# Constant products in the waits of four layer normalisations of a decoder step

## The chip, the cores and the metric

The kernel runs on one core of a Trainium2 chip. The metric is the time of one execution on the device in microseconds (us), as the median of several runs. All inputs and outputs lie in the chip's memory, in float32.

## The reference

One step of a two-layer decoder. Layer 0 is a convolution module and an MLP; layer 1 is attention with stick-breaking weights and an MLP. Both run for a prompt of 512 tokens and for 8 samples of 4 tokens with 2048 past keys each. Every sub-layer ends in the same normalisation:

```python
def post_norm_residual(x, y, gate, g, b):
    return layer_norm(DEEPNORM_ALPHA * x + (1.0 + gate) * y, g, b)

def layer_norm(x, g, b):
    mu = mean(x, -1);  var = mean(square(x - mu), -1)
    return (x - mu) * rsqrt(var + LN_EPS) * g + b
...
h = x * (1.0 + scale) + shift            # ahead of each sub-layer
y = square(relu(h @ mlp_w1)) @ mlp_w2    # the MLP
```

The convolution module has a `layer_norm` of its own between its depthwise convolution and its last projection. The model's width is 1024, the MLP's 4096.

## The kernel before

The prompt's activations lie transposed: eight tiles `v` of 128 channels by 512 tokens. A dense layer multiplies 128 x 128 blocks of weights with these tiles into a PSUM bank `pd`. For precision every factor is split into a high and a low part (`whi`, `wlo`, `xhi`, `xlo`, or `h2h`, `h2l` in the MLP), and `mm3` issues three products for each pair of blocks, in lines 311, 314 and 315. `wsplit` makes the parts of the weights, `split` and `make_h` those of the activations.

A normalisation has to work across channels, which lie across partitions. `Norm.add` transposes each finished tile of `v` by TensorE into a bank `lnT` (line 350), and VectorE takes its statistics (`bn_stats`). After the last tile `Norm.bands` does three things. It aggregates the statistics. It spreads the mean over all partitions: `spread` makes diagonal matrices `dg` out of the means (on VectorE for the even blocks of 128 tokens, on ScalarE for the odd ones) and multiplies them by `onesm`, a matrix of ones, into a bank `mb`. And it works out the reciprocal deviation by a Newton iteration of small VectorE instructions (`rstd_of`) and spreads that into a bank `rb` in the same way. In line 370 stand all these products. `make_h` then subtracts `mb` from each tile and multiplies it by `rb` (lines 404 and 405, VectorE), makes `xhi` and `h` on ScalarE (lines 438 and 440) and `xlo` on VectorE (line 444).

Four normalisations of the prompt are concerned. They are called here C (in the convolution module, object `cnrm`), 0A (behind the convolution module), 0B (behind the first MLP) and 1A (behind the attention). C and 0B treat all 512 tokens at once. 0A and 1A go in two halves of 256 tokens (`H_0A = H_1A = 1`), with mean and deviation of a half side by side in one bank `mrb`. The first half is normalised while the last tiles of the second half are still being made, and its first products, 48 of 256 columns in `p_tiles`, are issued as soon as `make_h` has its tiles; `second_half` starts the second half's.

Two streams of work are interleaved, the prompt's and the samples' (`ada_A`, `sd_acc`, `w_acc`, `zt`, `av` belong to the latter), by a clock of costs that the generators yield. Behind that a scheduler puts the instructions of each engine into one order, by a simulated time line, priorities (the statistics run under `high_priority`) and dependences through tiles; `order` adds a dependence between two instructions that has no semaphore and sets the order alone. The banks of PSUM are three for `pm` (products, and `mrb` of a first half or `rb`), four for `aux`, and one for `ln`.

Of the kernel before, what the change touches and what calls it, by code (L numbers as in the profile page):

```python
# [17 lines left out]
P = 128  # L18
# [92 lines left out]
def yoco_step_kernel(  # L111
# [10 lines left out]
    mm = nc.tensor.matmul  # L122
    tr = nc.tensor.transpose
# [17 lines left out]
    def pm(name="pm"):  # L141
        return ps.tile([P, 512], F32, tag="pm", bufs=3, name=name)
# [30 lines left out]
    ident = c1[:, 0:128]  # L173
# [5 lines left out]
    onesm = base.tile([P, P], F32, name="onesm")  # L179
# [40 lines left out]
    pt = aux("pt_c")  # L220
# [96 lines left out]
    def order(ins, after):  # L317
        tc.add_manual_dep(ins.ins, after.ins.name,
                          mybir.DependencyInfo(mybir.DependencyClass.NoSync, mybir.DependencyReason.DATA), reason="issue order")
        return ins  # L320
# [16 lines left out]
    axd = [dr.tile([KT, P, T], F32, name=f"axd{i}") for i in range(2)]  # L337

    class Norm:
        def __init__(self, n=4, pl4=None, psum=None):  # L340
            self.n, self.psum, self.first, self.after = n, psum, None, None
            self.st = pp.tile([P, 4, KT, 6], F32, tag="bn", bufs=1, name="bn") if n == 4 else pl4.tile(
                [P, n, KT, 6], F32, tag="bn2", bufs=2, name="bn2")

        def add(self, v, k, ts=None, keep=None):
            blocks = range(self.n) if ts is None else range(ts.start // P, ts.stop // P)
            with tc.high_priority(LN_PRI):
                pt = (self.psum or lnp)("lnT")
                for i in blocks:
                    tr(pt[:, i * P : i * P + P], v[:, i * P : i * P + P], ident)  # L350
                for i in blocks:
                    vec.bn_stats(self.st[:, i, k, :], pt[:, i * P : i * P + P])  # L352
            if keep is not None:
                for i in blocks:
                    nc.scalar.copy(keep[i], pt[:, i * P : i * P + P])
# [21 lines left out]
        def bands(self, ts):  # L377
            if self.first and ts.start == 0:
                return self.first
            b0, b1 = ts.start // P, ts.stop // P  # L380
            with tc.high_priority(LN_PRI):
                mv = self.aggregate(range(b0, b1))
                if b1 - b0 == 4:
                    mb, rb = lnp("mb"), pm("rb")
                else:
                    both = (lnp if b0 else pm)("mrb")
                    mb, rb = both[:, 0:256], both[:, 256:512]
                self.spread(mv[:, b0:b1, 0], mb)
                self.spread(rstd_of(mv[:, b0:b1, 1], b1 - b0), rb)
                return mb, rb  # L390

    ALL = slice(0, T)

# [14 lines left out]
    last_spread = []  # L408

    def rstd_of(var, n):  # L410
        ve = stmp([P, 32], "ve", tag="ln0")[:, 0:n]
        vh = stmp([P, 32], "vh", tag="ln3")[:, 0:n]
        y = stmp([P, 32], "rs", tag="ln1")[:, 0:n]
        w = stmp([P, 32], "rw", tag="ln2")[:, 0:n]
        vec.tensor_scalar_add(ve, var, EPS)
        vec.tensor_scalar(w.bitcast(I32), ve.bitcast(I32), 1, None, op0=ALU.logical_shift_right)
        vec.tensor_scalar(y.bitcast(I32), w.bitcast(I32), -1.0, float(0x5F3759DF), op0=ALU.mult, op1=ALU.add)
        vec.tensor_scalar_mul(vh, ve, -0.5)
        for _ in range(3):
            vec.tensor_tensor(w, y, y, op=ALU.mult)  # L420
            vec.tensor_tensor(w, w, vh, op=ALU.mult)
            last_rstd[:] = [vec.scalar_tensor_tensor(y, w, 1.5, y, op0=ALU.add, op1=ALU.mult)]
        return y
# [175 lines left out]
    for h in range(2):  # L599
        acc = aux("ada_A00")  # L600
        for kk in range(4):
# [3 lines left out]
            for g in range(4):  # L605
                mm(acc[32 * g : 32 * g + 32, :], cT[:, 2 * kk + g // 2, :], blk[:, g * 512 : g * 512 + 512],
                   start=(kk == 0), stop=(kk == 3), tile_position=(0, 32 * g))
# [4 lines left out]
    pt = aux("pt_p")  # L612
# [42 lines left out]
    sfull = sl.tile([P, KT, NS, CW + 3], F32, name="sfull")  # L655
    su = sfm("su", "su")
    y = vtiles()
    cnrm = Norm()
    raw = {}


# [76 lines left out]
    for c in range(4):  # L738
# [3 lines left out]
        for o in range(2):  # L742
            sacc = aux("pw1s")
            for r in range(2):
                for g in range(4):
                    k = 2 * g + r
                    mm(sacc[32 * g : 32 * g + 32, 0:256], s_h[:, k, :], st[o][:, k, :], start=(r == 0),
                       stop=(r == 1), tile_position=(0, 32 * g))
# [4 lines left out]
        for o in range(2):  # L753
            for i in range(2):
                mm(us[:, o * 64 + i * 32 : o * 64 + i * 32 + 32], sps[o][:, i * P : i * P + P], sel4,
                   start=True, stop=True)
# [13 lines left out]
        if c == 0:  # L770
# [11 lines left out]
            for j in range(4):  # L782
                n = (CW - j + 3) // 4
# [320 lines left out]

    def p_tiles(w, xh, xl, nk, ts=ALL, hold=None):
        out = [pm("pd")[:, 0 : ts.stop - ts.start] for _ in w]
        for k in range(nk):
            for a, (hi, lo) in zip(out, w):
                mm3(a, hi[:, k, :], lo[:, k, :], xh[k][:, ts], xl[k][:, ts], k == 0, k == nk - 1,
                    hold[1] if hold and hold[0] == k else None)  # L1110
        return out
# [68 lines left out]
    def prompt():  # L1180
# [6 lines left out]
        for c in range(2):  # L1187
            pt = aux("ucT")
# [28 lines left out]
        yield from need("gB0")  # L1217
        yield from need("abA01")
        v = vtiles()
        nrm = Norm()  # L1220

        def resid(l, s, i):
            ax = {}
# [14 lines left out]
        a9, b9 = mods["abA01"]  # L1238
        hl = make_h(v, lambda k: a9[:, k, 8:9], lambda k: b9[:, k, 8:9], nrm, H_0A)
        yield LN_COST  # L1240
        nrm = Norm()
        yield from p_mlp(*hl, v, 0, nrm, H_0A, H_0B)
        xhi, xlo = make_h(v, lambda k: pcol(R_LNG + 1, k), lambda k: pcol(R_LNB + 1, k), nrm, H_0B)
        yield LN_COST
# [31 lines left out]
        for c in range(4):  # L1276
            st = wstage(w_kv[:, D + c * 256 : D + c * 256 + 256], KT)
            ws = [wsplit(st[:, 4 * r : 4 * r + 4, :], 0, 256) for r in range(2)]
            for i2 in range(2):
                a = pm("pv")  # L1280
                for ii in range(2):
                    i = i2 * 2 + ii
# [32 lines left out]
        for pr in range(KT):  # L1315
# [5 lines left out]
            for unit in units:  # L1321
# [13 lines left out]
                for i, c0 in unit:  # L1335
                    for r, z in zip(halves, zs):
                        order(mm(z[:, c0 : c0 + (i + 1) * P], qT[r, i * P : i * P + P], kT[r, 0 : (i + 1) * P], start=False,
                                 stop=False, skip_group_check=True), head)
# [34 lines left out]
        yield from need("gB1")  # L1373
        yield from need("abA11")
        v = vtiles()
        nrm = Norm()
        yield from p_dense_out(attn_wo[0], ohi, olo, resid(1, 0, 1), last=H_1A)
        a9, b9 = mods["abA11"]
        hl = make_h(v, lambda k: a9[:, k, 8:9], lambda k: b9[:, k, 8:9], nrm, H_1A)
        nrm = Norm()  # L1380
# [47 lines left out]
    while any(alive):  # L1428
        i = 0 if (alive[0] and (not alive[1] or clock[0] <= clock[1])) else 1
# [42 lines left out]
```

## Time and profile before

| | us |
|---|---|
| median of 3 runs | 1671.01 (1669.94 to 1671.44) |
| the profiled execution | 1672.76 |
| its span, first to last instruction | 1671.0 |
| TensorE busy | 1564.6 (94%) |
| VectorE busy | 956.5 (57%) |
| ScalarE busy | 568.6 (34%) |
| granted TensorE clock, mean | 0.974 of 2.4 GHz |

PE is TensorE, PEld its loading of weights, DVE VectorE, ACT ScalarE, POOL GpSimd, SP the engine that issues most transfers. PEclk is the granted clock of TensorE as a share of 2.4 GHz: 1.00 is 2.4 GHz, 0.50 is 1.2 GHz, and values between are means over a stretch that has both. A product of two float32 operands shows in the trace as two records, so the count of records is higher than that of products in the code. The products of line 311, 314 and 315 show as one record each.

### The profile page before, as it was taken

The numbers are of one execution on the slowest core, as the hardware profiler recorded it, in microseconds if no ns is written. First come the engines' busy times: TensorE is split into PE (matmuls) and PEld (weight loads), VectorE is DVE, ScalarE is ACT, GpSimd is POOL, SyncE is SP. The second block draws the span as 40 slices with busy tenths as digits, with TensorE's granted clock in tenths as the row PEclk, the third lists the DMA queues.
The fourth block names the chain that finished last, engine by engine and source line by source line (L and its number), as shares of the span: only waits on it lengthen the run. The fifth ranks groups of instructions, "written<-read, shape, count | busy, mean of one in ns | idle before, by whom it ended". The sixth has DMA issues, their size and how long they took to land.

```text
span 1671.0 us, 25460 instructions
## 1 busy us (share of the span) xinstructions
PE 1564.6 (94%) x10489; PEld 1090.3 (65%) x10489; DVE 956.5 (57%) x1812; ACT 568.6 (34%) x903; POOL 188.4 (11%) x221
## 2 busy tenths in 40 slices
PE   4899988989999999999899999889889999999995
PEld 2566424656777777777468775546777767556885
DVE  2399637385576755655643457975774533332546
ACT  1322105153332332323332444852272323223332
POOL 4100110000112111110012112021101000000002
PEclk9899999989999999999999999999999999999998
DMA  8787879878676866576879878355546585995221
GB/s 292 247 294 265 265 230 393 318 261 309 235 267 243 322 227 234 218 279 227 318 271 316 296 239 325 134 213 185 192 162 244 184 312 180 356 346 191 85 70 51
DMA packets 152968, 409.25 MB, mean 245 GB/s; under 512 B 8807, under 2 KB 82823, under 8 KB 128261
## 3 DMA queue, kind: packets, MB, share of 16 engines
q1 hardware_dynamic: 48739, 159.76, 25.7%
q0 software_dynamic: 23584, 149.07, 24.7%
q10 hardware_dynamic: 80530, 98.80, 17.8%
q8 instruction: 82, 1.34, 0.3%
q14 instruction: 33, 0.27, 0.0%
HBM read 390.57 MB, written 17.88 MB: 244 GB/s over the span
## 4 chain that ended last, share of the span: by engine, by line
PE 73%; issue 10%; DVE 8%; DMA 6%; ACT 1%; POOL 1%; SPq 0%; DVEq 0%; ACTq 0%; POOLq 0%
PE pd L311 17%; PE pd L315 17%; PE pd L314 17%; PE zt L1001 3%; PE av L1052 3%; PE sd_acc L535 2%; PE cv L693 2%; DMA stage<-in_conv_pw_w_dram 2%; PE w_acc L562 1%; DVE v L670 1%; PE ada_A L237 1%; PE lnT L350 1%; DMA kraw<-in_cache_k_dram,krow 1%; PE pw L311 1%; PE pw L314 1%
## 5 line engine op out<-in xcount | busy, mean ns | idle before, releaser
L305 DVE TENSOR_TENSOR wlo<-stage,whi 128x1024 fp32r<-128x1024 f32 x184 | 223.3, 1217 | 252.2 <-ACT whi L304 251.8
L304 ACT CAST whi<-stage 128x1024 fp32r<-128x1024 f32 x184 | 191.6, 1046 | 423.1 <-PE pd L315 353.1
L311 PE MATMUL pd<-xhi,whi 128*128 128x512 f32 (+1 forms) x832 | 321.0, 387 | 11.3 <-ACT whi L304 5.5
L314 PE MATMUL pd<-xhi,wlo 128*128 128x512 f32 (+1 forms) x832 | 318.9, 384 | 2.1 <-DVE wlo L305 2.0
L315 PE MATMUL pd<-xlo,whi 128*128 128x512 f32 (+1 forms) x832 | 313.0, 387 | 5.5 <-DVE xlo L444 5.0
L995 DVE STREAM_TRANSPOSE kt<-kraw 128x512 f32<-128x512 f32 x256 | 164.3, 685 | 123.7 <-DMA kraw<-in_cache_k_dram,krow 84.0
L311 PE MATMUL pd<-h2h,whi 128*128 128x512 f32 (+1 forms) x544 | 206.7, 388 | 1.6 <-DVE v L1170 1.0
L315 PE MATMUL pd<-h2l,whi 128*128 128x512 f32 (+1 forms) x544 | 205.2, 383 | 0.0
L314 PE MATMUL pd<-h2h,wlo 128*128 128x512 f32 (+1 forms) x544 | 204.9, 381 | 0.0
L311 PEld LDWEIGHTS pd<-xhi,whi 128*128 128x128 f32 x832 | 161.1, 194 | 60.9 <-issue 14.3
L315 PEld LDWEIGHTS pd<-xlo,whi 128*128 128x128 f32 x832 | 157.0, 193 | 58.4 <-issue 15.4
L314 PEld LDWEIGHTS pd<-xhi,wlo 128*128 128x128 f32 x832 | 161.0, 193 | 42.8 <-issue 12.7
L1170 DVE SCALAR_TENSOR_TENSOR v<-pd,mod_B,v 128x512 f32<-128x512 f32 x120 | 87.8, 745 | 115.8 <-PE pd L315 115.4
L973 POOL DMA_INDIRECT kraw<-in_cache_k_dram,krow x64 | 65.9, 1029 | 631.1 <-DVE kt L995 396.0
L311 PEld LDWEIGHTS pd<-h2h,whi 128*128 128x128 f32 x544 | 101.9, 188 | 34.6 <-issue 10.4
L1145 ACT ACTIVATE relu<-pd 128x512 f32<-128x512 f32 (+1 forms) x68 | 38.9, 572 | 240.3 <-PE pd L315 235.1
L315 PEld LDWEIGHTS pd<-h2l,whi 128*128 128x128 f32 x544 | 101.8, 188 | 28.6 <-issue 9.4
L314 PEld LDWEIGHTS pd<-h2h,wlo 128*128 128x128 f32 x544 | 102.2, 188 | 25.2 <-issue 6.7
L973 POOL DMA_INDIRECT vt<-in_cache_v_dram,vrow x64 | 67.0, 1047 | 273.7 <-PE av L1052 235.3
L1001 PE MATMUL zt<-kt,qb 128*32 128x128 f32 x2048 | 77.0, 280 | 5.2 <-DVE kt L995 5.2
L1001 PEld LDWEIGHTS zt<-kt,qb 128*32 128x32 f32 x2048 | 53.4, 111 | 30.3 <-issue 14.7
L352 DVE BATCH_NORM_STATS2 bn<-lnT 128x6 f32<-128x128 f32 x160 | 36.5, 285 | 62.4 <-PE lnT L350 62.2
(299 smaller groups left out, 2014.6 us busy)
## 6 DMA issues: line engine op xcount, KB each, us to landing
sw<-in_mlp_w_dram SPq DMA_DIRECT2D x64, 1024.0 KB
stage<-in_mlp_w_dram ACTq DMA_DIRECT2D x64, 1024.0 KB
adaw<-in_ada_w_dram SPq DMA_DIRECT2D x40, 1024.0 KB
stage<-in_conv_pw_w_dram ACTq DMA_DIRECT2D x12, 1024.0 KB
adaw<-in_ada_w_dram SPq DMA_DIRECT2D x16, 512.0 KB
swkv<-in_w_kv_dram SPq DMA_DIRECT2D x8, 1024.0 KB
stage<-in_w_kv_dram ACTq DMA_DIRECT2D x8, 1024.0 KB
ur<-ud POOLq DMA_DIRECT2D x24, 270.0 KB, 7.5
```

Of the source, the lines that this page charges most:

```text
L304: nc.scalar.copy(hi, st[:, :, c0 : c0 + cw])
L305: vec.tensor_tensor(lo, st[:, :, c0 : c0 + cw], hi.bitcast(F32), op=ALU.subtract)
L311: first = mm(out, whi, xh, start=start, stop=False)
L314: mm(out, wlo, xh, start=False, stop=False)
L315: latest[:] = [mm(out, whi, xl, start=False, stop=stop)]
L352: vec.bn_stats(self.st[:, i, k, :], pt[:, i * P : i * P + P])
L973: nc.gpsimd.indirect_dma_start(out=out, out_offset=None, in_=cache.rearrange("g (r e) h d -> (g r) (e h d)", e=2), in_offset=bass.Indirect ...
L995: ins = vec.transpose(kt[:, 2 * x : 2 * x + 2, :], raw[x].rearrange("p (e c) -> p e c", e=2)[:, :, c0 : c0 + 256])
L1001: behind(mm(zt[u][32 * g : 32 * g + 32, f * P : f * P + P], qb[:, u, hh * 8 + bl].rearrange("p x q -> p (x q)"), kt[:, :, bl * 32 : bl * 3 ...
L1052: behind(mm(av[32 * g : 32 * g + 32, :], wT[u][:, i, e, a, :], vt[:, e * D + u * 512 : e * D + u * 512 + 512], start=(a == 0 and i == 0), ...
L1145: latest_act[:] = [act(r, a, AF.Relu)]
L1170: ins = vec.scalar_tensor_tensor(v[kt][:, ts], a, gt[:, kt, 8:9], v[kt][:, ts], op0=ALU.mult, op1=ALU.add)
```

## The change

`Norm` gets three numbers, `fill`. `bands` issues so many products of `onesm` with itself (128 x 128) into the bank `mb` ahead of the spread of the mean, so many into `rb` ahead of the spread of the deviation, and leaves the third number in a list `waiting`, from which the next `p_tiles` issues so many into its first bank ahead of its own products. Each is ordered behind the one before it, the first of each group behind the last transposition or behind the last product of the spread. Nobody reads these results: the spread, and the products with `start=True`, write the same places anew. In a normalisation of two halves only the second half (`b1 == 4`) gets them.

```diff
-        def __init__(self, n=4, pl4=None, psum=None):
-            self.n, self.psum, self.first, self.after = n, psum, None, None
+        def __init__(self, n=4, pl4=None, psum=None, fill=(0, 0, 0)):
+            self.n, self.psum, self.first, self.after, self.fill = n, psum, None, None, fill
...
-                    tr(pt[:, i * P : i * P + P], v[:, i * P : i * P + P], ident)
+                    self.last = tr(pt[:, i * P : i * P + P], v[:, i * P : i * P + P], ident)
...
+                whole = b1 == 4
+                idle_products(mb, self.fill[0] * whole, self.last)
                 self.spread(mv[:, b0:b1, 0], mb)
+                idle_products(rb, self.fill[1] * whole, last_spread[0])
                 self.spread(rstd_of(mv[:, b0:b1, 1], b1 - b0), rb)
+                if whole:
+                    waiting[:] = [(self.fill[2], last_spread[0])]
                 return mb, rb
+
+    waiting = []
+
+    def idle_products(out, n, after):
+        for _ in range(n):
+            after = order(mm(out[:, 0:P], onesm, onesm, start=True, stop=True), after)
...
-    cnrm = Norm()
+    cnrm = Norm(fill=(3, 3, 6))
...
         out = [pm("pd")[:, 0 : ts.stop - ts.start] for _ in w]
+        while waiting:
+            idle_products(out[0], *waiting.pop())
         for k in range(nk):
...
-        nrm = Norm()
+        nrm = Norm(fill=(8, 0, 2))
...
-        nrm = Norm()
+        nrm = Norm(fill=(4, 5, 4))
...
-        nrm = Norm()
+        nrm = Norm(fill=(4, 0, 5))
```

The last three are 0A, 0B and 1A. The order of the instructions on an engine is fixed when the kernel is built. On TensorE at norm 0A it was this before, from the second half's last transposition (`lnT`) to its spread of the deviation (the last `mrb`); `smp` and `urow` belong to the samples, and where rows are left out the 48 products of the first half go on, with the spread of the mean among them:

```order
L350 MATMUL lnT<-c_82,v 128x128 x2
L311 MATMUL pd<-xhi,whi 128x256
L314 MATMUL pd<-xhi,wlo 128x256
L548 MATMUL w_t<-c_82,sd_sb 128x2x32 x4
L315 MATMUL pd<-xlo,whi 128x256 x2
...
L499 MATMUL smp<-sred,meanm 128x32
L732 MATMUL urow<-c_82,su 32x128 x8
L237 MATMUL ada_A_2645<-adaw,cT 32x512 x4
L370 MATMUL mrb<-dg,onesm 128x128 x2
```

In the changed kernel, at the same place, from the last transposition to the first products of the first half:

```order
L350 MATMUL lnT<-c_82,v 128x128 x2
L560 MATMUL w_t<-c_82,sd_sb 128x2x32 x4
L402 MATMUL mrb<-onesm 128x128 x8
L370 MATMUL mrb<-dg,onesm 128x128 x2
L511 MATMUL smp<-sred,meanm 128x32 x2
L744 MATMUL urow<-c_82,su 32x128 x8
L370 MATMUL mrb<-dg,onesm 128x128 x2
L237 MATMUL ada_A_2657<-adaw,cT 32x512 x4
L402 MATMUL pd<-onesm 128x128 x2
L311 MATMUL pd<-xhi,whi 128x256
L314 MATMUL pd<-xhi,wlo 128x256
L315 MATMUL pd<-xlo,whi 128x256
```

All 48 products of the first half have moved behind both spreads of the second half. At norm 1A it is the same, with four and five of the new products. On ScalarE at norm 1A it was this before, from the second half's last diagonal on; `relu` and `h2h` are the first half's, `xhi` and `h` the second's:

```order
L367 ACTIVATE dg<-c_82,rs 128x128
L1145 ACTIVATE relu<-pd 128x256
L1146 ACTIVATE relu_10633<-relu 128x256
L1145 ACTIVATE relu<-pd 128x256
L327 CAST h2h<-relu_10633 128x256
L1146 ACTIVATE relu_10641<-relu 128x256
L327 CAST h2h<-relu_10641 128x256
L438 ACTIVATE xhi<-v,b_A_7056,a_A_7055 128x256
L440 ACTIVATE h<-v,b_A_7056,a_A_7055 128x256
```

And now:

```order
L367 ACTIVATE dg<-c_82,rs 128x128
L450 ACTIVATE xhi<-v,b_A_7091,a_A_7090 128x256 x4
L1159 ACTIVATE relu<-pd 128x256
L1160 ACTIVATE relu_10677<-relu 128x256
L1159 ACTIVATE relu<-pd 128x256
L327 CAST h2h<-relu_10677 128x256
L1160 ACTIVATE relu_10685<-relu 128x256
L452 ACTIVATE h<-v,b_A_7091,a_A_7090 128x256
L327 CAST h2h<-relu_10685 128x256
L452 ACTIVATE h<-v,b_A_7091,a_A_7090 128x256 x3
```

The first half's `relu` and `h2h` now stand among the second half's `xhi` and `h`, behind four `xhi`. VectorE's `h2l` of the first half, which stood ahead of the second half's subtractions at both places (and at 0A ahead of its last diagonal), now stands behind four pairs of them.

## Rows read from the trace of the kernel before

**Rows 1.** The page: busy time of TensorE over the span, and the chain's shares by engine.

```profile
PE 1564.6 (94%) x10489; PEld 1090.3 (65%) x10489; DVE 956.5 (57%) x1812; ACT 568.6 (34%) x903; POOL 188.4 (11%) x221
...
PE 73%; issue 10%; DVE 8%; DMA 6%; ACT 1%; POOL 1%; SPq 0%; DVEq 0%; ACTq 0%; POOLq 0%
```

**Rows 2.** Windows of the span; columns: window, length, each engine's busy time, PEclk, DMA share, GB/s.

```profile
249.00:269.00 20.00, 13.97 (x98) 6.03 (x96) 16.78 (x45) 12.07 (x20) 0.00 (x0) 1.00 1.01 412
353.00:358.00 5.00, 1.82 (x16) 0.64 (x13) 5.00 (x32) 2.27 (x7) 0.00 (x0) 1.00 0.09 17
358.00:366.00 8.00, 7.18 (x33) 3.87 (x34) 7.76 (x23) 5.73 (x12) 0.00 (x0) 0.58 0.86 303
827.20:834.00 6.80, 6.24 (x18) 3.20 (x18) 6.63 (x12) 6.67 (x10) 0.00 (x0) 0.51 1.03 403
1226.40:1229.70 3.30, 3.24 (x15) 3.24 (x16) 3.20 (x11) 3.30 (x8) 0.00 (x0) 0.50 0.41 174
372.50:815.00 442.50, 441.42 (x3067) 321.85 (x3066) 265.58 (x418) 139.50 (x197) 57.80 (x56) 1.00 0.71 255
```

**Rows 3.** Timeline of TensorE at norm 0A; columns: start, length, instruction, [idle before it <- releaser].

```profile
345.27 0.41 PE L311 MATMUL pd<-xhi,whi 128*128 128x256 f32 x1
345.48 0.41 PE L314 MATMUL pd<-xhi,wlo 128*128 128x256 f32 x1
...
352.17 0.28 PE L311 MATMUL pd<-xhi,whi 128*128 128x256 f32 x1
352.29 0.28 PE L314 MATMUL pd<-xhi,wlo 128*128 128x256 f32 x1
...
358.16 0.71 PE L370 MATMUL mrb<-dg,onesm 128*128 128x128 f32 x4 [3.34 <-DVE dg L369]
358.81 1.46 PE L237 MATMUL ada_A<-adaw,cT 128*32 128x512 f32 x8
...
371.31 1.06 PE L237 MATMUL ada_A<-adaw,cT 128*32 128x512 f32 x8
372.31 0.50 PE L315 MATMUL pd<-xlo,whi 128*128 128x256 f32 x2
```

**Rows 4.** Timeline of VectorE at norm 0A.

```profile
355.02 0.40 DVE L330 TENSOR_TENSOR h2l<-relu,h2h 128x256 fp32r<-128x256 f32 x1
...
357.83 0.28 DVE L369 TENSOR_SCALAR dg<-c,rs 128x128 f32<-128x128 f32 x1
```

**Rows 5.** Timeline of TensorE at norm 1A.

```profile
1219.11 1.92 PE L1052 MATMUL av<-vt,wT 128*32 128x512 f32 x16
1220.96 0.71 PE L370 MATMUL mrb<-dg,onesm 128*128 128x128 f32 x4
...
1232.31 0.40 PE L315 MATMUL pd<-xlo,whi 128*128 128x256 f32 x2
```

**Rows 6.** Timeline of all engines at norm 1A.

```profile
1218.12 0.29 DVE L369 TENSOR_SCALAR dg<-c,rs 128x128 f32<-128x128 f32 x1
...
1219.16 0.38 ACT L1145 ACTIVATE relu<-pd 128x256 f32<-128x256 f32 x1 [0.64 <-PE pd L315]
...
1220.90 0.41 ACT L327 CAST h2h<-relu 128x256 fp32r<-128x256 f32 x1
...
1222.62 0.60 ACT L438 ACTIVATE xhi<-v,b_A,a_A 128x256 fp32r<-128x256 f32 x1 [1.31 <-DVE v L405]
...
1223.13 0.59 ACT L440 ACTIVATE h<-v,b_A,a_A 128x256 f32<-128x256 f32 x1
```

**Rows 7.** Timeline of all engines at norm 0B.

```profile
832.66 0.68 DVE L444 TENSOR_TENSOR xlo<-h,xhi 128x512 fp32r<-128x512 f32 x1
...
835.20 0.73 PE L315 MATMUL pd<-xlo,whi 128*128 128x512 f32 x2
```

**Rows 8.** Timeline of VectorE at norm C.

```profile
257.77 0.69 DVE L405 TENSOR_TENSOR v<-v,rb 128x512 f32<-128x512 f32 x1 [2.12 <-PE rb L370]
```

**Rows 9.** Waits of TensorE: who waited for whom, total us, times, longest.

```profile
PE zt L1001 <- DVE kt L995: 5.2, 3, 2.2
```

## The prediction

> **What bounds the kernel now.** I read the page first: TensorE is busy 94% of the span, and the chain that ended last lies on it for 73% [rows 1]. Then the windows: from 372.5 to 815 us TensorE is busy 441.42 of 442.50 us at a clock of 1.00 [rows 2], so there is no gap in which a delay could be made good; what a normalisation adds to TensorE's time moves the end. What the change can win or lose therefore stands in four places: the normalisations C (after the convolution), 0A, 0B and 1A. The reader is to see there which stretches ran at half clock: 358 to 366 us (0A, mean 0.58), 827.2 to 834 (0B, 0.51) and 1226.4 to 1229.7 (1A, 0.50); at C the clock stays at 1.00 from 249 to 269 us although TensorE is busy only 13.97 of 20 us [rows 2]. Ahead of the stretch at 358 us TensorE had been busy 1.82 us in five [rows 2].
>
> The timelines then tell who is waited for. At 0A and 1A the products come in two halves of 256 columns, 48 products each (16 in each of the lines L311, L314, L315). TensorE's last wait at 0A is 3.34 us for the diagonal that VectorE makes from the second half's statistics [rows 3], and VectorE is busy all of 353 to 358 us [rows 2]. While VectorE works those statistics out, TensorE runs the first half's 48 products. That is the cover that stands there already.
>
> **The change part by part.** It adds 44 fillers (12 at C, 10 at 0A, 13 at 0B, 9 at 1A) and moves nothing by intent. A filler is a 128-column product like those of the spread: a row of four records, which are two products, takes 0.71 us [rows 5], so 0.36 us each; all 44 would be 16 us if nothing covered them. Where they stand in the queue matters more. At 0A and 1A the last group is issued into the bank of the first half's products, after the last spread of the second half. Those 48 products write the same bank, so they now stand behind the second half's statistics, which they used to cover. That is the hold. The order of the change shows it on TensorE, and on ScalarE it shows the relu of the first half moved from ahead of the second half to behind four of its eight xhi.
>
> *Norm 0A.* The second half's spread needs the diagonal of 357.83 [rows 4]. Two h2l of 0.40 us leave VectorE's queue ahead of it, the first at 355.02 [rows 4], so it comes 0.8 earlier: the spread ends at 358.16 - 0.8 + 0.7 = 358.1 [rows 3]. Then TensorE has one ada group (1.46 [rows 3]), two fillers (0.7), and the 48 held products with two ada groups among them (1.06 each [rows 3]). Their pitch is 0.12 us at 2.4 GHz (352.17 to 352.29) and 0.21 at 1.2 GHz (345.27 to 345.48) [rows 3]. All 48 are 5.8 us or 10.1 us. I take 16 at half clock, as many as fill a stretch of 3.3 us, the length of that at 1226.4 [rows 2], and 32 at full clock: 3.4 + 3.8 = 7.2. The first half ends at X = 358.1 + 1.5 + 0.7 + 7.2 + 2.1 = 369.6. Behind X stand 48 products of the second half and four ada groups, 5.8 + 4.2 = 10.0, so the second half ends at 379.6. Before, it ended at 372.8 [rows 3]. Two ada groups more than before have been done by then, 2.1 us of work that is not due later. So 379.6 - 372.8 - 2.1 = **+4.7 us**. All at full clock: X = 358.1 + 1.1 + 0.5 + 5.8 + 2.1 = 367.6, and +2.7. All at half clock: X = 374.9, and +10.0. The eight fillers ahead of the first spread are hidden: they stand behind the last transposition, where the first half's products were.
>
> *Norm 1A.* The diagonal is written at 1218.4 [rows 6], but before the spread ran only at 1220.96, behind the first half and 1.92 us of av [rows 5]. Now it comes at 1218.4 and ends at 1219.1. This is a gain of 2.4 us for VectorE. Then five fillers (1.8) and the held 48 (7.2): X = 1228.1. Behind X the path goes through ScalarE, whose relu waits for the bank and holds what is queued behind it: relu to the second h2h took 1219.16 to 1221.31, 2.15 us [rows 6]; then come four h, and four times xhi and h, 12 instructions that start 0.5 apart (1222.62 to 1223.13 [rows 6]), 6.0 us; then the last xlo and the last products, 0.8. X + 9.0 = 1237.1, against 1232.7 before [rows 5]: **+4.4 us**. Full clock: X = 1226.1, +2.4; half clock throughout: X = 1231.9, +8.2. No ada group is credited here; av and the zt products are the same in number before and after.
>
> *Norm 0B.* It has no halves, and nothing is held. The fillers keep TensorE busy up to the first product, so the half-clock stretch of 6.8 us [rows 2] may go. What is late next is VectorE: the second xlo is written at 833.34, and TensorE used it at 835.20 [rows 7], so no more than 1.9 us can be had before TensorE waits for VectorE instead. I take **-1.2 us**, between 0 and that limit and nearer to it because the stretch ends just there; bounds -1.9 and +0.4 (one filler more than the wait holds).
>
> *Norm C.* The clock is full already, so nothing can be won. Three fillers stand ahead of the spread of rb, for which VectorE waited 2.12 us [rows 8]: between 0 and 3 x 0.36 = 1.1 us late. TensorE idles 6 of these 20 us, so I take **+0.3 us**. The six behind the spread lie in that idle time; without it they would be 2.2 us.
>
> Sum: 0.3 + 4.7 - 1.2 + 4.4 = +8.2 us. The profiled execution took 1672.76 us, 1.75 more than the median 1671.01; on it the sum gives 1681.0, and on the median **1679.2 us**. The low ends give 0 + 2.7 - 1.9 + 2.4 = +3.2 (1674.2), the high ends 1.1 + 10.0 + 0.4 + 8.2 = +19.7 (1690.7).
>
> On the hold, the row at 1220.96 is what I go by: a ready spread stood 2.6 us behind products queued ahead of it [rows 5, 6]. The Trainium skill (TensorE: Matmul & The Clock Gate, section The mechanism) says that matmuls start and end strictly in program order. By that rule the trace agrees, and the hold is unavoidable; without it TensorE could pass the fillers, and the sum would be 0.3 - 1.2 = -0.9.
>
> **The rivals.** *The clock is what counts* (faster). If the fillers keep the clock up and the held products cost nothing because VectorE ends the half anyway, the half-clock stretches return 8.0 x 0.42 + 6.8 x 0.49 + 3.3 x 0.50 = 8.3 us at most [rows 2], and the time is 1662.7. For it: TensorE was idle ahead of the stretch at 358 us. Against it: ScalarE and VectorE have the first half's relu and h2l in the middle of their second half, so they can't end it before X. It decides from X below 364.9 at 0A (372.8 + 2.1 - 10.0), and the sum puts X at 367.6 even at full clock. The Trainium skill (the same page, section HAM oscillation) says that idle gaps between bursts of products throw the clock back to half; by that rule filling them is right, and the time would go towards this rival. The trace shows a fall after the idle time at 0A, and none at C.
>
> *The delay is absorbed* (no change). TensorE waits 5.2 us in all for transposed keys in the attention [rows 9]. If those waits shrink because TensorE comes later, 8.2 - 5.2 = 3.0 is left: 1674.0. Against it: VectorE's instructions there are fed by the same delayed prompt, and the wait is in three pieces of up to 2.2 us.
>
> *All held products run at half clock* (slower still): the high ends, up to 1690.7. For it: between its eight fillers and the spread at 0A TensorE has little to do. Against it: stretches of 3.3 to 8 us are all that the rows show.
>
> *The change doesn't do what it says.* The eight fillers at 0A stand right behind the last transposition and ahead of the spread of the mean, not in the wait of 353 to 358 us, and so cover little. This is part of the forecast.
>
> **How the numbers follow.** A measurement of this kernel can tell about 0.2%, 3.3 us. The forecast, 1674.4 to 1687, has 0.72; more than that 0.07; absorbed 0.13; faster 0.08. So faster 0.08, same 0.13, slower 0.79. A range of 1673 to 1687 leaves out the faster case, most of the cold one and part of the absorbed one.
>
> **What would show it.** In the changed kernel the first half's 48 products at 0A start after the second half's spread of rb, near 360 us, and at 1A near 1221. ScalarE's first relu there waits for TensorE, and VectorE's h2l for ScalarE. The second halves end 5 to 7 us later at 0A (with two more ada groups done) and some 4 us later at 1A. At 0B the clock stays at 1.00, and the gain is near 1 us; at C nothing moves. I am wrong if the first half still runs under the statistics, if X lies within 2 us of the second half's end as it was, or if a stretch behind 1233 us makes the delay good.

## The result and the profile after

The changed kernel takes 1681.56 us in the median of 7 runs (1675.59 to 1682.20), the kernel before 1671.32 beside it (1669.94 to 1673.08). The ratio is 1.0056, with a 95% interval of 1.0044 to 1.0067: slower by 9.4 us (7.4 to 11.2). The forecast was 1679.2 us with a range of 1673 to 1687, so time and sign came as forecast. Two of its terms did not, and it lacks one thing; these errors nearly cancelled, and the runs below separate them.

The page of the changed kernel's profiled execution (1681.56 us, span 1679.8), to be read against [rows 1]: TensorE is busy 6.6 us longer, and the chain has 13% "issue" where it had 10%.

```profile
PE 1571.2 (94%) x10577; PEld 1100.0 (65%) x10577; DVE 956.1 (57%) x1812; ACT 569.3 (34%) x903; POOL 191.7 (11%) x221
...
PE 71%; issue 13%; DMA 7%; DVE 6%; POOL 1%; ACT 1%; ACTq 0%; DVEq 0%; POOLq 0%
```

Windows of the changed kernel (window, length, busy time of PE, PEld, DVE, ACT, POOL, then PEclk, DMA share, GB/s), at C, at 0A ahead of the held products and over them, at 0B, and at 1A. They answer to [rows 2].

```profile
249.60:269.60 20.00, 16.58 (x122) 8.95 (x122) 16.55 (x45) 11.89 (x20) 0.00 (x0) 1.00 1.01 407
341.00:361.40 20.40, 12.04 (x52) 8.96 (x52) 19.12 (x86) 8.23 (x18) 0.00 (x0) 0.61 0.61 242
361.40:369.40 8.00, 8.00 (x63) 6.04 (x60) 1.42 (x4) 1.76 (x3) 0.00 (x0) 0.93 0.86 321
837.90:844.70 6.80, 4.54 (x29) 2.13 (x27) 6.66 (x12) 6.52 (x10) 0.00 (x0) 1.00 1.03 405
1222.50:1230.50 8.00, 8.00 (x54) 8.00 (x55) 3.10 (x8) 2.46 (x5) 0.00 (x0) 0.78 0.01 2
```

The third row is the hold seen from the other engines: TensorE is busy without a gap, and VectorE has 1.42 us of work in 8, ScalarE 1.76; in [rows 2], 358 to 366 us, VectorE had 7.76. Work that used to run side by side now runs one after the other. The fourth row is 0B. The clock is 1.00 there, as the change intends, but TensorE is busy only 4.54 of 6.80 us, where it had been busy 6.24 at a clock of 0.51.

TensorE at 0A in the changed kernel, to be read against [rows 3]:

```profile
343.82 3.73 PE L402 MATMUL mrb<-onesm 128*128 128x128 f32 x16
...
358.40 1.22 PE L370 MATMUL mrb<-dg,onesm 128*128 128x128 f32 x4 [2.98 <-DVE dg L369]
359.55 1.94 PE L237 MATMUL ada_A<-adaw,cT 128*32 128x512 f32 x8
361.41 1.20 PE L402 MATMUL pd<-onesm 128*128 128x128 f32 x4
362.29 0.44 PE L311 MATMUL pd<-xhi,whi 128*128 128x256 f32 x1
362.57 0.28 PE L314 MATMUL pd<-xhi,wlo 128*128 128x256 f32 x1
362.69 0.28 PE L315 MATMUL pd<-xlo,whi 128*128 128x256 f32 x1
...
370.44 0.28 PE L315 MATMUL pd<-xlo,whi 128*128 128x256 f32 x1
...
381.29 0.40 PE L315 MATMUL pd<-xlo,whi 128*128 128x256 f32 x2
```

The first half's 48 products start at 362.29, behind the second half's spread, and the last of them starts at 370.44; before, they were under way at 345.27. The wait for the diagonal is still there (2.98 us, before 3.34): the fillers did not fill it. ScalarE and VectorE, in the same place, wait for those products:

```profile
370.46 0.39 ACT L1159 ACTIVATE relu<-pd 128x256 f32<-128x256 f32 x1 [6.93 <-PE pd L315]
...
371.89 0.43 DVE L330 TENSOR_TENSOR h2l<-relu,h2h 128x256 fp32r<-128x256 f32 x1 [9.00 <-ACT h2h L327]
```

1A shows the same, TensorE first, then the relu that waits for it [rows 5, 6]:

```profile
1222.49 1.22 PE L370 MATMUL mrb<-dg,onesm 128*128 128x128 f32 x4 [4.66 <-DVE dg L369]
1223.50 2.34 PE L402 MATMUL pd<-onesm 128*128 128x128 f32 x10
...
1231.45 0.28 PE L315 MATMUL pd<-xlo,whi 128*128 128x256 f32 x1
...
1231.47 0.38 ACT L1159 ACTIVATE relu<-pd 128x256 f32<-128x256 f32 x1 [3.85 <-PE pd L315]
...
1241.14 0.40 PE L315 MATMUL pd<-xlo,whi 128*128 128x256 f32 x2
```

### The profile page after: what moved, and what is told of

The parts are those of the page before. It is cut to its first block, busy times and chain, and to the rows that moved or that the text cites. A ratio compares the mean times of both kernels' runs of the same rounds, so it can differ in the third digit from the quotient of the medians.

```text
span 1679.8 us, 25633 instructions
## 1 busy us (share of the span) xinstructions
PE 1571.2 (94%) x10577; PEld 1100.0 (65%) x10577; DVE 956.1 (57%) x1812; ACT 569.3 (34%) x903; POOL 191.7 (11%) x221
## 3 DMA queue, kind: packets, MB, share of 16 engines
q10 hardware_dynamic: 80530, 98.80, 17.6%
## 4 chain that ended last, share of the span: by engine, by line
PE 71%; issue 13%; DMA 7%; DVE 6%; POOL 1%; ACT 1%; ACTq 0%; DVEq 0%; POOLq 0%
PE pd L311 16%; PE pd L315 16%; PE pd L314 16%; PE zt L1013 3%; PE sd_acc L547 2%; PE cv L705 2%; PE av L1064 2%; DMA kraw<-in_cache_k_dram,krow 2%; DMA stage<-in_conv_pw_w_dram 2%; PE w_acc L574 2%; DMA ur<-ud 1%; PE ada_A L237 1%; PE pw L314 1%; PE pw L311 1%; PE pw L315 1%
## 5 line engine op out<-in xcount | busy, mean ns | idle before, releaser
L314 PE MATMUL pd<-xhi,wlo 128*128 128x512 f32 (+1 forms) x832 | 315.5, 380 | 1.5 <-DVE wlo L305 1.5
L315 PE MATMUL pd<-xlo,whi 128*128 128x512 f32 (+1 forms) x832 | 312.5, 382 | 2.9 <-DVE xlo L456 2.1
L315 PE MATMUL pd<-h2l,whi 128*128 128x512 f32 (+1 forms) x544 | 205.1, 383 | 0.0
L315 PEld LDWEIGHTS pd<-xlo,whi 128*128 128x128 f32 x832 | 155.9, 190 | 56.8 <-issue 17.7
L314 PEld LDWEIGHTS pd<-xhi,wlo 128*128 128x128 f32 x832 | 158.1, 190 | 39.3 <-issue 10.8
L315 PEld LDWEIGHTS pd<-h2l,whi 128*128 128x128 f32 x544 | 101.7, 188 | 30.1 <-issue 10.9
```

What stands on the lines that cost most here:

```text
L314: mm(out, wlo, xh, start=False, stop=False)
L315: latest[:] = [mm(out, whi, xl, start=False, stop=stop)]
```

## The experiments

Two theories stood at the start. The first: the loss is the hold, which comes from the bank of the third filler group at 0A and 1A. The rival: the fillers cost by themselves, by their own time or by what they do to the clock. All kernels compute the whole result. The comments in the edits are added here. Times are medians; "+" is the ratio's distance from 1 times 1671.4 us, with its interval.

### The hold, without and alone

`e1_no_third` takes the third group away at 0A and 1A:

```diff
-        nrm = Norm(fill=(8, 0, 2))      # 0A
+        nrm = Norm(fill=(8, 0, 0))
...
-        nrm = Norm(fill=(4, 0, 5))      # 1A
+        nrm = Norm(fill=(4, 0, 0))
```

> This kernel is the changed one without the third filler group at 0A and 1A (two and five products), so that the first half's 48 products are no longer queued behind the second half's spread; the other 37 fillers stay. Theory (the hold is the loss): the half-clock stretch at 0B stays filled, the halves run as they did before, and the time comes out at 1670 to 1672 us, about one microsecond under the kernel before; the second halves at 0A and 1A end within 1 us of the kernel before. Rival (the fillers themselves cost, by their own time or by what they do to the clock): 37 of 44 fillers are still there, so most of the loss stays, 1677 to 1680 us.

Measured: 1671.41 us beside 1671.43, ratio 0.9998 (0.9986 to 1.0009). The loss is gone although 37 of the 44 fillers are still there.

`e2_hold_only` is the other side: one filler at each place, in the first half's bank.

```diff
-    cnrm = Norm(fill=(3, 3, 6))         # C
+    cnrm = Norm()
...
-        nrm = Norm(fill=(8, 0, 2))      # 0A
+        nrm = Norm(fill=(0, 0, 1))
...
-        nrm = Norm(fill=(4, 5, 4))      # 0B
+        nrm = Norm()
...
-        nrm = Norm(fill=(4, 0, 5))      # 1A
+        nrm = Norm(fill=(0, 0, 1))
```

> This kernel is the one before with a single filler at 0A and a single one at 1A, each put into the first half's bank behind the second half's last spread; C and 0B have none. Theory (the hold is the loss): all of it stays, 6 us at 0A and 5 at 1A, without the gain at 0B of about 1 us: 1680 to 1684 us. Rival (the fillers themselves cost): two products of less than 0.5 us each are left, so 1671 to 1672 us.

Measured: 1680.03 us, ratio 1.0046 (1.0028 to 1.0063), +7.7 us. Two products that nobody reads cost nearly the whole loss. The first theory stands and its rival falls.

`e7_second_bank` keeps all 44 fillers and changes the bank of the third group alone:

```diff
-        while waiting:
+        while waiting and ts.stop == T:     # in halves: the second half's bank
             idle_products(out[0], *waiting.pop())
```

> This kernel is the changed one with all 44 fillers, only that at 0A and 1A the third group is put into the first bank of the second half's products in place of the first half's. Theory (the bank is the loss, not the products): the first half runs under the statistics again, and the seven products cost at most their own 2 to 3 us: 1670 to 1674 us. Rival (what costs is that products stand behind the last spread, in whatever bank): 1679 to 1682 us, as the changed kernel.

Measured: 1673.32 us, ratio 1.0006 (0.9998 to 1.0015), +1.0 us. The profile has the first half's products ahead of the spread again, and the two fillers still behind it:

```profile
353.30 0.40 PE L315 MATMUL pd<-xlo,whi 128*128 128x256 f32 x2
...
359.12 0.71 PE L370 MATMUL mrb<-dg,onesm 128*128 128x128 f32 x4 [3.41 <-DVE dg L369]
359.67 0.85 PE L402 MATMUL pd<-onesm 128*128 128x128 f32 x4
```

With the same products behind the same spread, but in a bank that has to wait for that spread anyway, nearly all of the loss is gone. It is the bank.

### The parts one by one

`e3_0A_alone` and `e4_1A_alone` have the change at one place each.

```diff
+        nrm = Norm(fill=(8, 0, 2))      # e3: 0A alone, the others Norm()
+        nrm = Norm(fill=(4, 0, 5))      # e4: 1A alone, the others Norm()
```

> This kernel has the change at 0A alone (eight fillers ahead of the first spread and two behind the last one). Theory (the parts add up, each by what its own place shows): the second half at 0A ends 6 us later with two more ada groups done taken off, and that reaches the end: 1676 to 1679 us. Rival (a delay is made good or made worse behind the place where it arises, since TensorE's waits in the attention stage move with it): the place shows 6 us, and the end differs from that by 3 us or more.

> This kernel has the change at 1A alone (four fillers ahead of the first spread and five behind the last one). Behind 1A the kernel has hardly a wait left (3.9 us in all, the same in both traces). Theory (the parts add up): the second half at 1A ends 5 us later and so does the kernel: 1675 to 1678 us. Rival (the fillers' own time is what counts): nine fillers of 0.25 to 0.47 us, 2 to 4 us, of which the four ahead of the spread stand in a wait: 1672 to 1674 us.

Measured: 0A alone 1674.17 us, 1.0015 (1.0006 to 1.0025), +2.5; 1A alone 1676.52 us, 1.0031 (1.0015 to 1.0046), +5.2. At 1A the theory holds. At 0A the end moves far less than the place does, and less than the theory of that run had: the second half ends some 9 us later, and 7 are left at 0B (table below). Something behind it gives back 4 to 5 us.

`e5_0B_alone` and `e6_C_alone`:

```diff
+        nrm = Norm(fill=(4, 5, 4))      # e5: 0B alone
+    cnrm = Norm(fill=(3, 3, 6))         # e6: C alone
```

> This kernel has the change at 0B alone (four, five and four fillers). Theory (a small gain, capped by VectorE): the half-clock stretch behind the normalisation goes, TensorE then waits for the second xlo, and the end comes 1 us earlier, 1670 to 1671 us. Rival (the clock is worth its full 3.3 us there): 1668 us. Rival (the fillers cost as much as they bring): 1671 to 1673 us.

> This kernel has the change at C alone (three, three and six fillers). Theory (nothing to win and nearly nothing to lose there): 1671 to 1672 us. Rival (twelve products on TensorE's path, 12 x 0.25 us): 1674 us.

Measured: 0B alone 1671.65 us, 0.9999 (0.9988 to 1.0010), -0.2; C alone 1670.68 us, 0.9993 (0.9979 to 1.0006), -1.2. Neither can be told from no change. At 0B the profiles say why. Three of them, TensorE from the last transposition to the second pair's last products (L315, in its second row): the kernel before in a second profile, a kernel without fillers at 0B whose clock did not fall (`e3_0A_alone`), and the changed kernel.

```profile
820.32 0.66 PE L350 MATMUL lnT<-c,v 128*128 128x128 f32 x4
...
829.56 0.80 PE L311 MATMUL pd<-xhi,whi 128*128 128x512 f32 x1 [1.63 <-ACT xhi L438]
...
837.00 0.74 PE L315 MATMUL pd<-xlo,whi 128*128 128x512 f32 x2
```

```profile
827.49 0.66 PE L350 MATMUL lnT<-c,v 128*128 128x128 f32 x4
...
836.73 0.50 PE L311 MATMUL pd<-xhi,whi 128*128 128x512 f32 x1 [1.62 <-ACT xhi L450]
...
840.44 0.73 PE L315 MATMUL pd<-xlo,whi 128*128 128x512 f32 x2 [1.53 <-DVE xlo L456]
...
843.02 0.73 PE L315 MATMUL pd<-xlo,whi 128*128 128x512 f32 x2
```

```profile
829.21 0.66 PE L350 MATMUL lnT<-c,v 128*128 128x128 f32 x4
...
838.92 0.50 PE L311 MATMUL pd<-xhi,whi 128*128 128x512 f32 x1 [0.73 <-ACT xhi L450]
...
842.63 0.73 PE L315 MATMUL pd<-xlo,whi 128*128 128x512 f32 x2 [1.52 <-DVE xlo L456]
...
845.21 0.73 PE L315 MATMUL pd<-xlo,whi 128*128 128x512 f32 x2
```

The distances are 837.00 - 820.32 = 16.7 us at half clock, 843.02 - 827.49 = 15.5 at full clock without fillers, 845.21 - 829.21 = 16.0 with fillers. At full clock TensorE waits 1.5 us for VectorE's xlo, so 1.2 is all that the clock is worth. The fillers delay the first product by 0.5 (9.7 for 9.2 us behind the transposition) and take nearly half of it back. All 14 profiles fall into these three groups: 16.6 to 16.7 us where the stretch is 6.8 us at half clock, 15.5 in the six others without fillers at 0B, 16.0 in the five with them.

### A plain delay, and the order behind it

Was the loss at 0A absorbed by waits further on? `e9_delay` delays TensorE there and holds nothing:

```diff
+                if l == 0 and fb == 0 and c == 1:
+                    waiting.append(24)
...
+        while waiting:                          # in p_tiles, ahead of the third pair's first product
+            last = latest[0]
+            for _ in range(waiting.pop()):
+                last = order(mm(out[0][:, 0:P], onesm, onesm, start=True, stop=True), last)
```

> This kernel is the one before with a plain delay of TensorE behind 0A: 24 of the same small products, 24 x 0.25 = 6 us at full clock, issued ahead of the third pair's first product at about 382 us; nothing is held in front of it. Theory (a delay of layer 0 is partly made good in the attention stage, whose waits for VectorE and ScalarE shrink when TensorE comes later): the time rises by 2 to 4 us, to 1673 to 1676 us, and the attention stage behind 0B is shorter by the rest. Rival (what arises at 0A reaches the end in full, and the smaller loss with the change at 0A alone is something else): 1677 to 1678 us.

Measured: 1676.92 us, 1.0028 (1.0015 to 1.0040), +4.7. The profile shows the 24 products in three pieces, 2.84 + 2.05 + 1.16 us; 0B comes 3.6 us later than the mean of the kernels without a hold, which scatter by some 2 us around it. What was left at 0B reached the end, 4.7 us (2.5 to 6.7). The attention did not make it good (its stretch of `awt`, in the table below, is the longest of all), so my theory on this run fell.

What the kernels with the hold at 0A have besides is another order of TensorE's instructions in layer 1's attention: the scheduler has ordered it anew. `e1`, `e4`, `e5`, `e6`, `e7` and `e9` keep the order of the kernel before between the first and the last `awt` (the prompt's attention weights, transposed); `e2`, `e3` and the changed kernel do not, nor does `e8_gap`, which holds nothing. There eight fillers stand behind the first half's products, ahead of a spread that is issued later for it:

```diff
+                    with tc.high_priority(LN_PRI):
+                        idle_products(rb, n, latest[0])       # n = 8, behind the first half's products
+                        for o, dg in spreads:                 # the second half's spread of rb
+                            last_spread[:] = [mm(o, onesm, dg, start=True, stop=True)]
                     second_half()
```

> This kernel is the one before with eight fillers in TensorE's wait of 3.34 us at 0A: between the first half's products and the second half's spread of rb, whose two products are therefore issued later in the program; no other fillers. Theory (filling a wait can win if it holds nothing up): TensorE is busy up to the spread, the half-clock stretch from 358 to 366 us goes, 0 to 3 us are won there: 1668 to 1671 us. Rival (the clock does not rise for these products either, as it did not for the eight ahead of the first spread in the changed kernel): 1671 to 1673 us.

Measured: 1670.41 us, 0.9994 (0.9983 to 1.0004), -1.0. The clock did rise: window of this kernel from the spread on, for 358 to 366 us in [rows 2]:

```profile
361.86:369.86 8.00, 6.31 (x44) 3.07 (x44) 7.76 (x23) 5.74 (x12) 0.00 (x0) 1.00 0.81 288
```

The clock is 1.00 where it was 0.58, and VectorE, busy 7.76 of 8 us in both, sets the pace: its last xlo ends 9.8 us behind the spread in both profiles. What differs is what TensorE has left by then, 2.6 us for 4.1. So the higher clock was worth 1.5 us here (12.4 us from the spread to the second half's end, for 13.9). But the fillers lost as much ahead of the spread, and the second half ends 34.0 us behind the last transposition in both. They did not fill the wait, which is still 3.06 us. They stand ahead of the samples' product `smp`, and the step of VectorE that takes its result stands ahead of the prompt's reciprocal deviation in VectorE's queue. That step starts 16.0 us behind the last transposition (14.2 before); an h2l that ends at 357.00 stands ahead of it here, so an earlier `smp` alone would have won little:

```profile
355.00 1.95 PE L410 MATMUL mrb<-onesm 128*128 128x128 f32 x16
...
356.57 0.43 DVE L330 TENSOR_TENSOR h2l<-relu,h2h 128x256 fp32r<-128x256 f32 x1 [2.02 <-ACT h2h L327]
...
356.78 0.31 PE L519 MATMUL smp<-sred,meanm 128*128 128x32 f32 x2
...
357.12 0.19 DVE L435 TENSOR_SCALAR ve<-smp 128x32 f32<-128x32 f32 x1
...
362.02 0.71 PE L1145 MATMUL mrb<-dg,onesm 128*128 128x128 f32 x4 [3.06 <-DVE dg L370]
```

`e12_one_filler` is the same kernel with `n = 1`. One product, no hold, and the other order, the same as in `e8_gap` on TensorE, VectorE and ScalarE from the first to the last `awt`.

> This kernel is the one before with a single filler at 0A, between the first half's products and the second half's spread of rb (whose two products are issued later in the program for that). It holds nothing. What it has in common with the kernels that have the hold at 0A is the order of TensorE's instructions in layer 1's attention, which the scheduler sets otherwise as soon as something near 0A changes. Theory (that new order is what gives back part of the loss at 0A): the waits between the first and the last awt product are 14 to 16 us for 17.5 to 19.5, and the time falls by 2 to 4 us, to 1667 to 1669.5 us. Rival (the shorter attention in those kernels is the clock of their executions): 1670.5 to 1672 us.

Measured: 1666.78 us beside 1671.36, 0.9969 (0.9956 to 0.9982), -5.2 us: faster than both kernels, by more than expected. The clock explains a third of it at most: these runs have 0.977 in the mean, the kernel before beside them 0.975, and within its runs 0.001 of clock goes with 0.8 us at most. How much of the rest is the order is not shown, since `e8_gap` has the same order and gained 1.0 (at most 2.8). Of the 4 us between the two, 1.3 lie at 0A, where the last diagonal comes that much later in `e8_gap` (its second half ends 34.0 us behind the last transposition, that of `e12` 32.7, at a clock of 0.79 from the spread on); for the others no run here shows a cause. In `e12` VectorE's step follows `smp` at once:

```profile
353.80 0.38 PE L410 MATMUL mrb<-onesm 128*128 128x128 f32 x2
354.02 0.31 PE L519 MATMUL smp<-sred,meanm 128*128 128x32 f32 x2
...
354.37 0.19 DVE L435 TENSOR_SCALAR ve<-smp 128x32 f32<-128x32 f32 x1 [1.00 <-PE smp L519]
...
359.55 0.71 PE L1145 MATMUL mrb<-dg,onesm 128*128 128x128 f32 x4 [3.35 <-DVE dg L370]
```

TensorE's products from the first `awt` on, as compiled (tile, and how many stand in a row; `zt` and `av` are the samples', `awt`, `pz` and `oP` the prompt's):

```
before:  awt3 pz1  zt8 pz5  zt8 awt3 zt8 pz2 oP6 awt3 av4 zt4 pz6 awt3
e12:     awt1 zt2 pz1 zt1 awt2 pz5 awt3 zt16 pz2 oP6 awt3 av4 pz10 awt3
```

The samples' products lie elsewhere between the prompt's, and other waits are filled. Waits of TensorE from the first to the last `awt`, of the kernel before and of `e12`:

```profile
PE awt L1357 <- DVE as L1354: 6.7, 6, 2.3
PE zt L1001 <- DVE kt L995: 5.2, 3, 2.2
```

```profile
PE zt L1021 <- DVE kt L1015: 5.5, 4, 2.4
PE awt L1385 <- DVE as L1382: 2.5, 5, 1.0
...
PE oP L1393 <- ACT as L1374: 2.0, 1, 2.0
```

### The same kernels once more

`e10_before_again` and `e11_after_again` are second profiles of the two kernels, with no edit.

> This is the kernel before itself, profiled once more. Theory (the clock behind 0B and in layer 1's attention is a matter of the execution, not of the program): the stretch of 6.8 us at half clock behind 0B is shorter or gone, or the stretch from the first to the last awt product (129.0 us at a mean clock of 0.93 in the profile of before) differs by 2 us or more, with TensorE's instructions and waits the same. Rival (the program sets the clock): both come again, 6.8 us within half a microsecond, and 129 us within one.

> This is the changed kernel itself, profiled once more. Theory: what the fillers keep and what they hold is the same in every execution: clock 1.00 from the last transposition of 0B on, the second half at 0A ending 41.6 to 42.1 us after the last transposition there (33 without the hold), the second half at 1A ending 44 to 45 us after the first half's last transposition; the attention's stretch of awt again shorter than in the kernel before, by the waits (14.9 for 18.7 us), and by whatever clock this execution has. Rival (these numbers too change with the execution): any of them off by more than 1 us.

Of the kernel before (1671.04 us) half came out as the theory had it. The half-clock stretch behind 0B is there again, 6.8 us long, as the rival said. The stretch of `awt` is not the same: 125.34 us at 0.96 for 128.96 at 0.93, with TensorE's order the same and waits of 18.0 for 18.7. First the window of the first profile of before, then that of the second:

```profile
1018.43:1147.39 128.96, 111.34 (x1137) 70.63 (x1137) 108.04 (x190) 77.35 (x150) 19.31 (x18) 0.93 0.55 201
```

```profile
1020.27:1145.61 125.34, 108.67 (x1137) 68.37 (x1137) 108.12 (x190) 77.25 (x150) 18.97 (x18) 0.96 0.56 206
```

The changed kernel's second profile (1682.68 us) repeats the first at the norms: 42.7 for 42.3 us at 0A, 44.9 for 44.7 at 1A. The first is 0.6 above the range that I had given, and the waits of its `awt` stretch are 15.9, above the 14.9.

The pieces of all 14 profiles, in us. "0A to 0B": from the last transposition of the one to that of the other. "awt": first to last, with the mean clock and the sum of TensorE's waits. "1A": from the first half's last transposition to the end of the second half's products.

| | 0A to 0B | awt | clock | waits | 1A |
|---|---|---|---|---|---|
| before | 479.7 | 129.0 | 0.93 | 18.7 | 39.5 |
| e10, before again | 481.2 | 125.3 | 0.96 | 18.0 | 39.5 |
| e1, no third group | 480.6 | 123.7 | 0.97 | 17.7 | 39.3 |
| e4, 1A alone | 481.0 | 123.8 | 0.97 | 17.5 | **44.3** |
| e5, 0B alone | 480.0 | 126.2 | 0.96 | 18.3 | 39.7 |
| e6, C alone | 483.6 | 126.2 | 0.95 | 17.6 | 39.3 |
| e7, second bank | 481.9 | 126.6 | 0.96 | 18.9 | 39.5 |
| e9, delay | 484.4 | 130.2 | 0.93 | 20.3 | 39.6 |
| e8, gap | 480.1 | *125.7* | 0.93 | *15.4* | 37.4 |
| e12, one filler | 478.8 | *122.0* | 0.97 | *15.9* | 39.3 |
| e2, hold only | **485.8** | *119.1* | 1.00 | *15.5* | **43.6** |
| e3, 0A alone | **487.7** | *120.6* | 0.97 | *14.7* | 39.3 |
| after | **489.8** | *122.2* | 0.96 | *14.9* | **44.7** |
| e11, after again | **487.8** | *123.4* | 0.96 | *15.9* | **44.9** |

Bold: held there. Italic: the other order. The hold costs 487.8 - 480.7 = 7.0 us at 0A (means, without `e9`) and 44.4 - 39.2 = 5.2 at 1A. The other order takes 122.2 us for 126.4, 4.2 less in the mean, and 2.5 to 4 less at one clock (0.97: 121.3 for 123.8; 0.93: 125.7 for 129.6). But this stretch holds 26 records of TensorE fewer in the other order (1111 for 1137). From the last transposition of 0B to the first half's last at 1A, where the work is the same, it is 368.3 for 372.0 us, 3.7 less in the mean, and single profiles overlap (365.0 to 372.3, and 369.2 to 375.8).

## Why the prediction was right, and where it was not

**The hold, right in kind.** TensorE did not pass the fillers, the first half's relu and h2l waited for it, and the second half ended late at both places, as the steps had it. The Trainium skill (TensorE: Matmul & The Clock Gate, section The mechanism) says that matmuls start and end in program order; by that rule the trace agrees (products that were under way at 345 us in the kernel before [rows 3] start at 362.29, behind the fillers), and `e7_second_bank` shows that another bank lifts the hold.

**Norm 1A: +4.4 forecast, +5.2 at the place and at the end.** X, the end of the first half, was put at 1228.1. It came at 1231.7; less the 3.6 us by which this execution was late there (1196.85 for 1193.26 at the first half's last transposition), 1228.1. That X agrees is luck: less those 3.6 us the spread ended at 1220.1, 1.0 later than in the sum, since its diagonal came 0.4 later and it ran at half clock, and the 48 products took 6.2 us for 7.2, since nearly all ran at full clock. Behind X 9.8 us went by (to 1241.5) for 9.0. The path through the relu was the right one.

**Norm 0A: +4.7 forecast, 7.0 at the place.** This term was too small. X came 31.3 us behind the last transposition (370.7 - 339.4) for 30.8 in the sum, the second half took 11.0 behind X for 10.0, and in the kernels without the hold it ends 33.4 us behind that transposition in the mean where the profile of before had 34.0. That makes 42.3 - 33.4 = 8.9, of which 1.9 are given back up to 0B; the credit for the ada groups done early was put at 2.1. The diagonal that was to come 0.8 earlier came 0.35 earlier (18.66 us behind the last transposition for 19.01). I had taken 16 of the held products at half clock. In fact nearly all ran at full clock (pitch 0.12 us from 362.57 on), and what ran at half clock was ahead of them: the spread took 1.22 us, the ada group 1.94 and the two fillers 1.20, where the sum had 0.7, 1.5 and 0.7 (they overlap a little).

**Norm 0B: -1.2 forecast, nothing measured.** The failing step is the half-clock stretch taken as a property of the kernel. Of nine profiles without fillers there it was 6.8 us long in three (before twice, `e2`), shorter in two (`e4`, `e12`: mean clock 0.75 over the same 6.8 us) and absent in four; with fillers it is absent in all five. No single profile therefore shows that the fillers keep the clock up there. Where the stretch is shorter or absent anyway, the fillers cost 0.5 us. That VectorE is late next (wait of 1.5 us for xlo) was right, and is why even the long stretch is worth only 1.2.

**Norm C: +0.3 forecast, 0.** From the last transposition to the first product it is 16.3 to 16.7 us with fillers and without.

**What the sum lacked.** The change "moves nothing by intent", the prediction says, and it gave what happens between the norms no term. The scheduler moved the attention. With that order the attention is 3.7 to 4.2 us shorter in the mean of the profiles; two kernels that have it and no hold gained 5.2 us (3.0 to 7.4, `e12`) and 1.0 (-0.7 to 2.8, `e8_gap`). With the measured pieces the sum is 0 + 7.0 + 0 + 5.2 - 4.2 = +8.0, against 9.4 (7.4 to 11.2) measured. The forecast of +8.2 was near for a reason that was partly luck: 0A was 2.3 too small, 1A 0.8 too small, 0B 1.2 too good, and the order was missing with the other sign.

**The rivals.** The clock as what counts: it counts for less than its stretches, because VectorE is busy through them. At 0A 8 us at 0.58 were worth 1.5 us and at 0B 6.8 us at 0.51 were worth 1.2, of the 3.4 and 3.3 that this rival took, and the fillers cost 1.5 and 0.5 there; neither `e8_gap` nor `e5_0B_alone` can be told from the kernel before by its time. The Trainium skill (same page, section HAM oscillation) advises against idle gaps for the clock's sake. Here the clock behind the spread was 1.00 with the eight fillers of `e8_gap` although the gap of 3.06 us stayed, and with the eight of the changed kernel it was 0.61 from 341 to 361.4 us. Absorbed: the shape was there, since 0A's loss reached the end as 2.5, but not the reason. TensorE's waits for transposed keys did not shrink (5.2 us before [rows 9], 7.9 in the changed kernel), what a plain delay left at 0B passed through, and the kernels where the loss shrank are those with the other order. All held products at half clock: not seen; and its X of 374.9 and 1231.9 are more than the terms shown give (372.5 and 1231.0).

What stays open is what turns the scheduler to the new order. `e12` has it with one product more at 0A (and a spread issued later), `e1` and `e7` keep the old one with eight and ten, so my words that any change near 0A does it were wrong. Open is also how much of the spread of 119 to 130 us in the `awt` stretch is order and how much is the clock of that execution, and with it what the order is worth at the end.

## What to carry to other kernels

A product that nobody reads is not free if its bank belongs to one that could run: issue it where the bank's next user has to wait for the same event, or the filler's dependence becomes that user's. Before filling a stretch at half clock, look at who is busy in it; where another engine has no gap there, the clock buys only what TensorE has left to do when that engine is done. Look also at who waits for the products behind the fillers. And where a scheduler orders the program, compare the whole order of before and after, not the place of the edit alone, and test the new order by itself: the one kernel here that was clearly faster had it.

## What the runs showed of the hardware

The same instructions in the same order did not get the same clock. `e4_1A_alone` has TensorE's order of the kernel before up to 1A, and behind 0B the same 6.8 us ran at 0.75 where both profiles of before have 0.51 and 0.52; in the `awt` stretch the mean clock of one order went from 0.93 to 0.97, and its length from 130.2 to 123.7 us. The Trainium skill (TensorE: Matmul & The Clock Gate, section What's actually happening) says that the number of products at the low clock at a kernel's start varies from run to run of one kernel; the traces show the like in the middle of one. The eight fillers at 0A are an instance: up to them and beyond, TensorE's order is the same in `e1_no_third` and `e7_second_bank`, and they took 2.00 us at a clock of 1.00 in the one (from 341.40) and 3.46 us at 0.56 in the other (from 343.20). What one profile shows at half clock is thus a bound of what filling can win, not a row to count on.
